# Input projection as seven block products, with attention among them and gates and convolution results in DRAM

## The chip, the cores and the metric

One core of one Trainium2 chip runs the whole kernel. The metric is the device time of one execution in microseconds; a version's time is the median of its runs. Engine names are those of the profile: PE (TensorE, matmuls), PEld (its weight loads), DVE (VectorE), ACT (ScalarE), POOL (GpSimd), SP (the queue that issues nearly all DMAs).

## The reference

A bidirectional encoder of two layers on 512 tokens of width 1024, in float32. Per layer (cut to what is computed):

```python
h = rms_norm(x, g_pre_mix[l])
z = h @ w_in[l]                                   # 1024 -> 6656 columns
q, k, v, cb, cc, cx, ga, gb = jnp.split(z, splits, axis=-1)
q = partial_rope(q.reshape(b, s, N_HEADS, HEAD_DIM), cos, sin)
k = partial_rope(k.reshape(b, s, N_KV_HEADS, HEAD_DIM), cos, sin)
y_attn = band_attention(q, k, v, attn_sink[l]) @ w_attn_proj[l]   # |i-j| <= 128
y_conv = (cb * short_conv(cc * cx, conv_w[l])) @ w_conv_proj[l]   # 3 taps
mix = (jax.nn.sigmoid(ga) * y_attn + jax.nn.sigmoid(gb) * y_conv) @ w_out[l]
x = x + rms_norm(mix, g_post_mix[l])
h = rms_norm(x, g_pre_ffn[l])
f = (jax.nn.silu(h @ w_gate[l]) * (h @ w_up[l])) @ w_down[l]
x = x + rms_norm(f, g_post_ffn[l])
```

q and the gates ga, gb have 1024 columns each, k and v 256 each, cb, cc, cx 1024 each. The FFN is 2816 wide.

## The kernel before

**Three products per float32 product.** Every matrix product is made of float32r matmuls on a high and a low part: `mm3` (L174) issues high x low, low x high, high x high into one PSUM bank. The parts of weights come from `split_w` (L129): ACT casts a 128x512 piece to its high part, DVE subtracts to get the low part. A weight tile arrives by DMA in `raw` (3 buffers), its parts lie in `hl` tiles (8 buffers of 128 x 2 x 512).

**Column tiles of 128.** A projection makes one column tile of 128 at a time for all 512 tokens: `gemm_steps` (L179) loads a 1024x128 piece of weights, splits it in two halves, and issues 8 x 3 matmuls of 512 columns. The normed input stands transposed and split in `hT` (`turn`, L238).

**A layer's mixer.** Values and keys come first (keys by `gemm_half`, two halves of 256 tokens). Then `products()` (L734) makes, for c = 0..7, a query tile (`query_tile`, L600, with rotation by `rope`), three tiles of the convolution (`conv_job`, L698: cx, cc, cb), and then eight tiles of `conv_proj` (L727). Attention is cut into `pieces` (L744 to L761): scores of a head group and block (`scores`, matmul L627, DVE L632), `softmax`, transposes and split of the weights (`weights`, L661 and L207), and the value product (`values`, L674). The loop at L770 issues a piece and then some steps of `products()`, so that pieces are spread evenly among the projections, after a lead of 12 steps. Finally, for m = 0..7, the loop at L780 makes a gate_conv tile, a gate_attn tile and a tile of the attention projection, applies the sigmoids from PSUM, and keeps the merged tile for the output projection.

**A layer's FFN.** Gate and up projections are already made as pairs of column tiles (`Pair`, L360) by a seven-product block scheme. A pair's 1024 x 256 weights are four blocks (two column tiles by two halves of the contraction); the input is four blocks too (two halves of the contraction by two halves of the tokens). Seven products of sums of such blocks, each of 4 x 3 matmuls of 256 columns, take the place of eight. `Rights` (L303) holds the sums of the input, made once; `Pair.prep` makes the sums of the weights (DVE, L393) and their parts; `Pair.product` issues the matmuls and recombines the results from PSUM (L434 to L448). `orders` sets the order of the products of all pairs. `down` (L268) is the product of the output and the down projection with the norm behind it; its last weight rows are kept resident (5 and 6 of them) and used token tile by token tile.

**What sets the order.** Each engine works its own queue in order. The order in a queue is fixed when the program is built: a scheduler places the instructions by their dependencies and its own estimate of times, starting from the order in which the code issues them, except inside `in_order` blocks. Tiles come from pools of fixed buffers (`unit` 22, `t4` 6, `t2` 6 in the code), and eight PSUM banks.

Of the kernel before, what the change touches and what calls it, by code (L numbers as in the profile page):

```python
# [10 lines left out]
F32 = mybir.dt.float32  # L11
# [18 lines left out]
EPS = 1e-6  # L30
AHEAD = 5
LEAD = 12
# [35 lines left out]
def encoder(ctx: ExitStack, tc: tile.TileContext, a, out):  # L68
# [22 lines left out]
    def unit(shape, dtype=F32R):  # L91
        return up.tile(shape, dtype, tag="u4", bufs=22, name=nm("u4"))

    def t4(shape, dtype=F32):
        return sp.tile(shape, dtype, tag="t4", bufs=6, name=nm("t4"))

    def t2(shape, dtype=F32):
        return sp.tile(shape, dtype, tag="t2", bufs=6, name=nm("t2"))
# [14 lines left out]
    cw_rows = sp.tile([DEPTH * 3 * KT, P], F32, tag="t2", bufs=6, name="cw_rows")  # L113
# [12 lines left out]
    xd = [tc.dram_tile([T, D], F32, name=f"xd{i}") for i in range(2 * DEPTH - 1)]  # L126

# [18 lines left out]
    def hl_tile():  # L146
        return wp.tile([P, 2, 512], F32R, tag="hl", bufs=8, name=nm("hl"))

    def split_cols(raw, n):

        tiles = []
        for hf in range(2):
            hl = hl_tile()
            split_w(raw[:, hf * 512 : hf * 512 + 512], hl[:, 0], hl[:, 1])
            tiles.append(hl.rearrange("p a (k c) -> p a k c", c=n))
        per = 512 // n
        return lambda part, k: tiles[k // per][:, part, k % per]
# [20 lines left out]

    def gemm_steps(w, c0, xs):  # L179
# [3 lines left out]
        for k in range(KT):  # L183
            mm3(acc, hl(0, k), hl(1, k), xs(k, 0), xs(k, 1), k == 0, k == KT - 1)
            yield
# [8 lines left out]

    def gemm(w, c0, xs):
        return run(gemm_steps(w, c0, xs))

    def gemm_half(accs, hls, xs, h):

        ts = slice(h * 256, h * 256 + 256)  # L200
        for acc, hl in zip(accs, hls):
            for k in range(KT):
                mm3(acc[:, ts], hl(0, k), hl(1, k), xs(k, 0)[:, ts], xs(k, 1)[:, ts], k == 0, k == KT - 1)
# [33 lines left out]

    def turn(t, xs, hT):  # L238

        ts = slice(t * P, (t + 1) * P)  # L240
        for hf in range(2):
            pt = bank()
            for j in range(4):
                nc.tensor.transpose(  # L244
                    pt[:, j * P : (j + 1) * P], xs[:, (4 * hf + j) * P : (4 * hf + j + 1) * P], ident
                )
            ks = slice(4 * hf, 4 * hf + 4)
            split_to(hT[:, 0, ks, ts], hT[:, 1, ks, ts], pt.rearrange("p (k c) -> p k c", k=4))
# [43 lines left out]
    def h_tile():  # L292
        return up.tile([P, 2, KT, T], F32R, tag="h", bufs=1, name=nm("h"))

    def xs_of(hT):
        return lambda k, part: hT[:, part, k, :]
# [6 lines left out]
    class Rights:  # L303


        def __init__(self):
            self.h = up.tile([P, 4, 2, KH, TH], F32R, tag="h", bufs=1, name=nm("h"))
            self.ops = {p: (self.h[:, i, 0], self.h[:, i, 1]) for i, p in enumerate((1, 2, 3, 5))}
            self.x = {}

# [9 lines left out]

        def turn(self, t, xs):
            cs = slice(t % 2 * P, t % 2 * P + P)
# [8 lines left out]

# [11 lines left out]

        def put(self, p, src, cs):
            h, lo = self.op(p)
            split_to(h[:, :, cs], lo[:, :, cs], src)
# [12 lines left out]

    class Pair:  # L360


        def __init__(self, w0, w1, c0, r):
            self.w0, self.w1, self.c0, self.r = w0, w1, c0, r
            self.hl, self.done = {}, set()

            self.raw = [None, None]

        def load(self, n, raw):
            self.raw[n] = raw  # L370
            nc.sync.dma_start(
                raw.rearrange("p (k c) -> p k c", k=KT),
                (self.w0, self.w1)[n][:, self.c0 : self.c0 + P].rearrange("(k p) c -> p k c", p=P),
            )

        def need(self, p):
            if self.raw[0] is None:
                self.load(0, raw_tile())
            if self.raw[1] is None and p not in (2, 1):
                self.load(1, unit([P, 1024], F32))  # L380

        def prep(self, p):
# [6 lines left out]
            if p not in (2, 1):  # L389
                l21, l22 = self.raw[1][:, :512], self.raw[1][:, 512:]  # L390
            if p == 5:
                self.sums = [t2([P, 512]) for _ in range(2)]
            add = lambda out, x, y: nc.vector.tensor_tensor(out=out, in0=x, in1=y, op=ALU.add)  # L393
            if p == 2:
                src = l12
            elif p == 1:
                src = l11
            elif p == 4:
                src = l22
            elif p == 5:  # L400
                src = self.sums[0]
                add(src, l21, l22)
            elif p == 6:
                src = self.sums[1]
                add(src, self.sums[0], l11)
            elif p == 3:
                src = self.sums[0]
                add(src, self.sums[1], l12)
            else:
                src = self.sums[1]  # L410
                add(src, l11, l21)
# [4 lines left out]
        def product(self, p):  # L416
# [6 lines left out]
            elif p == 1:  # L423
                self.v = t4([P, 4, TH])
                self.g = self.v[:, 2:].rearrange("p a t -> p (a t)")
            acc = self.b if p == 2 else self.c if p in (5, 3) else self.a
            hl, (h, lo) = self.hl.pop(p), self.r.op(p)
            for k in range(KH):
                mm3(acc, hl[:, 0, k], hl[:, 1, k], h[:, k], lo[:, k], p in (2, 1, 5) and k == 0, k == KH - 1, p not in (2, 1, 5))
            if p != 2:  # L430
                r1 = v2 = self.v[:, 0]
                r5 = c22 = self.v[:, 1]
# [481 lines left out]
```

## Time and profile before

| | |
|---|---|
| median of 3 runs | 1673.93 us (1673.88 to 1674.6) |
| profiled execution | 1674.66 us, its span 1672.9 us |
| mean granted PE clock | 0.997 |
| DMA | 174.35 MB, mean 104 GB/s |

The profile's page gives the busy time of each engine, the chain of work that ended last, and groups of instructions by line with their mean duration and the idle time before them. Windows of time give the same per stage: the input projection and attention of layer 0 lie between about 30 and 340 us, its FFN's pairs between about 505 and 730 us. Matmuls are pipelined, so the distance between their starts, not their duration, is what one costs. The lines that matter are shown with the prediction.

### The profile page before, as it was taken

To read this page: it belongs to the slowest core of one execution; us is meant where nothing else is said; L and a number is where in the kernel's file an instruction comes from. 1 tells how busy PE (TensorE), PEld (TensorE's weight loads), DVE (VectorE), ACT (ScalarE), POOL (GpSimd) and SP (SyncE) were. 2 spreads that over 40 slices of the span, in tenths; PEclk is the share of its full clock that TensorE was granted. 3 is DMA by queue.
4 is the path that set the end of the run, shared out by engine and by line. 5 is a ranking of instruction groups with operands and counts; after the bars stand their busy time and mean duration, and the time that the engine had idled before them with its cause. 6 is when DMAs were issued, how large, how long until landed. Compare 5 with 4: busy or idle time off the path is not lost.

```text
span 1672.9 us, 24896 instructions
## 1 busy us (share of the span) xinstructions
PE 1650.1 (99%) x9457; PEld 1454.9 (87%) x9457; DVE 1141.8 (68%) x2230; ACT 862.7 (52%) x1806; POOL 72.3 (4%) x114
## 2 busy tenths in 40 slices
PE   7999999999999999999999999999999999999998
PEld 7888888888889999988898888888888899999886
DVE  6988876434469988854469788754434899888442
ACT  5566666433346655543346666564333555556331
POOL 0000000000011100000000000000000011001000
PEclk9999999999999999999999999999999999999999
DMA  6322222433452333343413222224335333434332
GB/s 201 94 76 76 65 87 64 133 95 101 129 161 76 102 102 101 115 138 127 150 64 101 76 76 76 76 76 126 101 100 164 101 92 99 108 103 133 111 115 76
DMA packets 246937, 174.35 MB, mean 104 GB/s; under 512 B 5488, under 2 KB 232864, under 8 KB 246816
## 3 DMA queue, kind: packets, MB, share of 16 engines
q1 hardware_dynamic: 246096, 171.18, 34.6%
q8 instruction: 74, 1.21, 0.3%
q10 hardware_dynamic: 720, 1.57, 0.3%
q14 instruction: 47, 0.39, 0.1%
HBM read 164.34 MB, written 8.39 MB: 103 GB/s over the span
## 4 chain that ended last, share of the span: by engine, by line
PE 97%; DVE 2%; ACT 1%; DMA 0%; POOL 0%; issue 0%; POOLq 0%; DVEq 0%; ACTq 0%
PE bank L176 30%; PE bank L177 30%; PE bank L175 30%; PE bank L627 2%; PE bank L674 2%; PE bank L661 2%; PE bank L244 0%; DVE u L207 0%; DVE h L207 0%; DMA t<-in_x_dram 0%; ACT t L228 0%; PE bank L327 0%; DVE t L264 0%; POOL r L222 0%; DVE t L236 0%
## 5 line engine op out<-in xcount | busy, mean ns | idle before, releaser
L175 PE MATMUL bank<-h,hl 128*128 128x256 f32 (+1 forms) x1536 | 521.6, 340 | 1.1 <-DVE h L207 1.1
L176 PE MATMUL bank<-h,hl 128*128 128x256 f32 (+1 forms) x1536 | 518.2, 337 | 0.0
L177 PE MATMUL bank<-h,hl 128*128 128x256 f32 (+1 forms) x1536 | 517.8, 337 | 0.0
L131 DVE TENSOR_TENSOR hl<-raw,hl 128x512 fp32r<-128x512 f32 x428 | 292.8, 693 | 230.9 <-ACT hl L130 228.3
L130 ACT CAST hl<-raw 128x512 fp32r<-128x512 f32 x428 | 261.6, 620 | 323.4 <-PE bank L177 241.5
L177 PEld LDWEIGHTS bank<-h,hl 128*128 128x128 f32 x1536 | 292.2, 190 | 30.9
L175 PEld LDWEIGHTS bank<-h,hl 128*128 128x128 f32 x1536 | 292.5, 190 | 29.3 <-DVE h L207 1.9
L176 PEld LDWEIGHTS bank<-h,hl 128*128 128x128 f32 x1536 | 292.5, 190 | 27.6
L175 PE MATMUL bank<-u,hl 128*128 128x256 f32 (+1 forms) x784 | 251.2, 321 | 3.4 <-DVE u L207 3.4
L176 PE MATMUL bank<-u,hl 128*128 128x256 f32 (+1 forms) x784 | 250.2, 319 | 2.7 <-ACT u L206 1.8
L177 PE MATMUL bank<-u,hl 128*128 128x256 f32 (+1 forms) x784 | 250.0, 319 | 0.0
L175 PEld LDWEIGHTS bank<-u,hl 128*128 128x128 f32 x784 | 149.7, 191 | 13.8 <-DVE u L207 3.8
L176 PEld LDWEIGHTS bank<-u,hl 128*128 128x128 f32 x784 | 149.9, 191 | 13.0 <-ACT u L206 2.2
L177 PEld LDWEIGHTS bank<-u,hl 128*128 128x128 f32 x784 | 150.0, 191 | 10.3
L130 ACT CAST hl<-t 128x512 fp32r<-128x512 f32 x176 | 108.3, 621 | 58.2 <-DVE t L393 41.1
L131 DVE TENSOR_TENSOR hl<-t,hl 128x512 fp32r<-128x512 f32 x176 | 133.4, 765 | 6.0 <-ACT hl L130 3.9
L175 PE MATMUL bank<-hl,u 128*128 128x512 f32 x304 | 118.3, 389 | 0.0
L176 PE MATMUL bank<-hl,u 128*128 128x512 f32 x304 | 118.3, 389 | 0.0
L177 PE MATMUL bank<-hl,u 128*128 128x512 f32 x304 | 118.3, 389 | 0.0
L647 ACT ACTIVATE t<-t,neg 128x256 f32<-128x256 f32 (+1 forms) x128 | 70.4, 552 | 21.1 <-DVE neg L642 20.8
L632 DVE CUSTOM_DVE_ANT_0 t<-bank,tab,sink 128x256 f32<-128x256 f32 (+1 forms) x128 | 65.7, 541 | 6.1 <-PE bank L627 5.9
L448 POOL TENSOR_TENSOR u<-t 128x256 f32<-128x256 f32 x44 | 51.9, 1179 | 397.4 <-DVE t L444 236.6
(123 smaller groups left out, 2121.4 us busy)
## 6 DMA issues: line engine op xcount, KB each, us to landing
raw<-in_w_in_dram SPq DMA_DIRECT2D x104, 512.0 KB, 3.9
u<-in_w_up_dram SPq DMA_DIRECT2D x44, 512.0 KB, 5.9
raw<-in_w_down_dram SPq DMA_DIRECT2D x44, 512.0 KB, 3.5
raw<-in_w_gate_dram SPq DMA_DIRECT2D x40, 512.0 KB, 4.0
raw<-in_w_conv_proj_dram SPq DMA_DIRECT2D x16, 512.0 KB, 4.2
raw<-in_w_attn_proj_dram SPq DMA_DIRECT2D x16, 512.0 KB, 4.3
raw<-in_w_out_dram SPq DMA_DIRECT2D x16, 512.0 KB, 3.5
xd<-t SPq DMA_DIRECT2D x12, 512.0 KB, 2.9
```

The costliest lines, as they stand in the source:

```text
L130: nc.scalar.copy(h, raw)
L131: eng.tensor_tensor(out=lo, in0=raw, in1=h.bitcast(F32), op=ALU.subtract)
L175: nc.tensor.matmul(acc, wh, xl, start=first, stop=False, skip_group_check=goes_on)
L176: nc.tensor.matmul(acc, wl, xh, start=False, stop=False, skip_group_check=goes_on)
L177: nc.tensor.matmul(acc, wh, xh, start=False, stop=last, skip_group_check=goes_on)
L448: nc.gpsimd.tensor_tensor(out=out[:, TH:], in0=c22, in1=self.g[:, TH:], op=ALU.mult)
L627: nc.tensor.matmul(s[:, :w], q, kk[g][:, 1 - part, lo_b * P : lo_b * P + w], start=part == 0, stop=part == 1)
L632: nc.vector.tensor_tensor_reduce(out=p, in0=s[:, :w], in1=mask[:, m0 : m0 + w], scale=HD**-0.5, scalar=sink[:, h : h + 1], op0=ALU.add, op ...
L647: nc.scalar.activation(p, p, AF.Exp, bias=neg[:, i : i + 1], accum_out=den[:, i : i + 1])
L661: nc.tensor.transpose(pt[:, i * P : (i + 1) * P], p[:, n * P : (n + 1) * P], ident)
L674: nc.tensor.matmul(o, v, hl[:, 1 - part], start=n == 0 and part == 0, stop=kb == hi_b and part == 1)
```

## The change

- All column tiles of the input projection except the values (25 pairs a layer: keys, 4 of queries, 8 of cx with cc, 4 of cb, 8 of gate_attn with gate_conv) become `Pair`s with seven block products. `Rights` takes the place of `hT`, and keeps one more plain block so that the value tiles can read it.
- In `Pair`, two of the four sums of weight blocks move from DVE to POOL (`need`); the products issue high x low and high x high for each of four blocks first, and the four low x high matmuls at the end.
- The pair's results are recombined in SBUF and handed to a subclass: rotation for keys and queries (the product with the sine on POOL), the convolution with its first product on POOL, the product with cb on POOL, and gates.
- Gates go to DRAM (`sgd`) unprocessed and convolution results go to DRAM (`cyd`); they are loaded again ahead of the merge and of `conv_proj`.
- Attention's pieces are spread by PE time spent (`FULL`, `HALF`), up to one tile before the end; the softmax works on two heads at a time; attention results stay in float32 and are split at the end.
- Buffers: `unit` 20, `hl` 6, `t4` 6, `t2` 8, and 4 of their own for the scores. `down` keeps 4 rows resident.

Its core:

```diff
+            if self.a1 is None:
+                l11, l21, l22 = self.raw[0][:, :512], self.raw[1][:, :512], self.raw[1][:, 512:]
+                self.a1 = t2([P, 512])
+                nc.gpsimd.tensor_tensor(out=self.a1, in0=l21, in1=l22, op=ALU.add)
+                nc.gpsimd.tensor_tensor(out=l21, in0=l21, in1=l11, op=ALU.add)
...
-    def gemm(w, c0, xs):
-        return run(gemm_steps(w, c0, xs))
...
             for k in range(KH):
-                mm3(acc, hl[:, 0, k], hl[:, 1, k], h[:, k], lo[:, k], p in (2, 1, 5) and k == 0, k == KH - 1, p not in (2, 1, 5))
+                nc.tensor.matmul(acc, hl[:, 0, k], lo[:, k], start=new and k == 0, stop=False, skip_group_check=not new)
+                nc.tensor.matmul(acc, hl[:, 0, k], h[:, k], start=False, stop=False, skip_group_check=not new)
+                yield HALF
+            for k in range(KH):
+                nc.tensor.matmul(acc, hl[:, 1, k], h[:, k], start=False, stop=k == KH - 1, skip_group_check=not new)
...
-            nc.vector.tensor_tensor(out=r2, in0=r2, in1=sin, op=ALU.mult)
+            nc.gpsimd.tensor_tensor(out=r2, in0=r2, in1=sin, op=ALU.mult)
...
+        class Conv(Pair):
+            def both(self):
...
+                nc.gpsimd.tensor_tensor(out=u[:, 1 : T + 1], in0=self.out0, in1=self.out1, op=ALU.mult)
...
+        class Outer(Pair):
+            def both(self):
+                for i, acc in enumerate((self.out0, self.out1)):
+                    c = 2 * self.n + i
+                    nc.gpsimd.tensor_tensor(out=ys[c], in0=ys[c], in1=acc, op=ALU.mult)
+                    nc.sync.dma_start(cyd[l][:, c], ys[c])
...
+        class Gates(Pair):
+            def both(self):
+                nc.sync.dma_start(sgd[l][:, self.m], self.v.rearrange("p a t -> p (a t)"))
...
+        order = [Keys(r, w_in, K0, w_in, K0 + P), queries(0), conv(0), queries(1), conv(1), outer(0)]
+        for n in (1, 2, 3):
+            order += [conv(2 * n), gates(2 * n - 2), conv(2 * n + 1), outer(n), gates(2 * n - 1)]
+            if n < 3:
+                order.append(queries(n + 1))
+        order += [gates(6), gates(7)]
...
         for m in range(KT):
-            acc = gemm(w_in, GB0 + m * P, xs)
...
+            sg = t4([P, 2, T])
+            nc.sync.dma_start(sg, sgd[l][:, m].rearrange("p (a t) -> p a t", a=2))
+            nc.scalar.activation(sg, sg, AF.Sigmoid)
+            nc.gpsimd.tensor_tensor(out=sg[:, 0], in0=sg[:, 0], in1=yc[m], op=ALU.mult)
```

How it moves instructions, at three places of layer 0. On PE, in the middle of the mixer, before: a tile of the convolution (`bank_1513`, weights `hl_1507`) with the value product, transposes and scores of attention among its wide matmuls:

```order
L175 MATMUL bank_1513<-h_86,hl_1507 128x512
L176 MATMUL bank_1513<-h_86,hl_1507 128x512
L177 MATMUL bank_1513<-h_86,hl_1507 128x512
L674 MATMUL bank_1464<-t_28_1472,u_0_92 128x512 x2
L661 MATMUL bank_1532<-ident,t_25_1343 128x128 x2
L661 MATMUL bank_1532<-ident,t_27_1400 128x128 x2
L627 MATMUL bank_1541<-u_3_445,u_10_841 128x384 x2
L627 MATMUL bank_1545<-u_3_445,u_10_841 128x384 x2
```

After: one product of a pair (`bank_1216`, weights `hl_1141`), again with attention inside it:

```order
L413 MATMUL bank_1216<-h_95,hl_1141 128x256
L414 MATMUL bank_1216<-h_95,hl_1141 128x256
L759 MATMUL bank_1219<-t_10_1100,u_0_96 128x512 x2
L742 MATMUL bank_1223<-ident,ps_790 128x128 x2
L742 MATMUL bank_1223<-ident,ps_853 128x128 x2
L413 MATMUL bank_1216<-h_95,hl_1141 128x256
L414 MATMUL bank_1216<-h_95,hl_1141 128x256
...
L417 MATMUL bank_1216<-h_95,hl_1141 128x256 x4
```

The matmuls of projections are half as wide, and a product of 12 of them needs one `hl` tile, where 24 wide ones needed two.

On POOL, in the same stage, before: only the zeros at the ends of the convolution's tiles stand there.

```order
L707 MEMSET t_15_702 128x1
L708 MEMSET t_15_702 128x1
L707 MEMSET t_22_984 128x1
L708 MEMSET t_22_984 128x1
L707 MEMSET t_31_1290 128x1
```

After: sums of weight blocks (L376, L377), the sine products of the rotation (L536) and the first product of the convolution (L584), each of 512 columns.

```order
L376 TENSOR_TENSOR t_16_825<-u_29_823 128x512
L377 TENSOR_TENSOR u_29_823<-u_29_823,raw_737 128x512
L582 MEMSET t_19_961 128x1
L583 MEMSET t_19_961 128x1
L584 TENSOR_TENSOR t_19_961<-t_7_386 128x512
L536 TENSOR_TENSOR t_18_935<-t_18_935,tab 128x512
L376 TENSOR_TENSOR t_21_988<-u_31_986 128x512
L377 TENSOR_TENSOR u_31_986<-u_31_986,raw_900 128x512
L536 TENSOR_TENSOR t_23_1131<-t_23_1131,tab 128x512
```

DVE or ACT, which work in order, read the results of each of them.

On DVE, before, at a query tile (`t_26`, rotation L505 to L508, low parts L606) between softmax and weights of attention:

```order
L505 STREAM_SHUFFLE t_27_1132<-bank_1057 128x512
L506 TENSOR_TENSOR t_26_1131<-bank_1057,tab 128x512
L650 TENSOR_TENSOR rd_1106<-den_1100,es_1098 128x4
L507 TENSOR_TENSOR t_27_1132<-t_27_1132,tab 128x512
L651 RECIPROCAL rd_1106<-rd_1106 128x4
L131 TENSOR_TENSOR hl_1361<-raw_1356,hl_1361 128x512
L656 TENSOR_SCALAR t_16_1033<-t_16_1033,rd_1106 128x256
L656 TENSOR_SCALAR t_18_1087<-t_18_1087,rd_1106 128x256
L508 TENSOR_TENSOR t_26_1131<-t_26_1131,t_27_1132 128x512
```

After, at a query tile (`t_17`, rotation L534, L535, L537, low parts L562), with low parts of weights (L135), a sum of weights (L393) and the convolution (L588):

```order
L534 STREAM_SHUFFLE t_18_935<-t_8_519 128x512
L535 TENSOR_TENSOR t_17_934<-t_8_519,tab 128x512
L135 TENSOR_TENSOR hl_945<-t_16_825,hl_945 128x512
L537 TENSOR_TENSOR t_17_934<-t_17_934,t_18_935 128x512
L588 SCALAR_TENSOR_TENSOR t_20_965<-t_19_961,cw,t_20_965 128x512
L393 TENSOR_TENSOR t_16_825<-t_16_825,raw_737 128x512
L562 TENSOR_TENSOR u_30_940<-t_17_934,u_30_940 64x512 x2
```

The product with the sine (L507 before) has left DVE; its sum (L537) stands two rows behind the shuffle that POOL's product needs, and the sources of the rotation are tiles in SBUF, no longer PSUM banks.

548 lines of the change are left out of this document (285 added, 263 removed).

## The prediction

> **What bounds the kernel now.** I read the page first: the busy line and the shares of the chain of waits.
>
> ```profile
> PE 1650.1 (99%) x9457; PEld 1454.9 (87%) x9457; DVE 1141.8 (68%) x2230; ACT 862.7 (52%) x1806; POOL 72.3 (4%) x114
> PE 97%; DVE 2%; ACT 1%; DMA 0%; POOL 0%; issue 0%; POOLq 0%; DVEq 0%; ACTq 0%
> ```
>
> The chain that ends last is 97% TensorE, so today a matmul less is time less. But a busy PE is pipelined, so its price per matmul is the distance between starts, not the duration. The timeline of PE shows it for 512 columns (first two rows, twelve steps apart) and for 256 columns (last two, twelve steps apart):
>
> ```profile
> 1206.34 0.39 PE L175 MATMUL bank<-h,hl 128*128 128x512 f32 x1
> ...
> 1209.06 0.39 PE L175 MATMUL bank<-h,hl 128*128 128x512 f32 x1
> ```
> ```profile
> 701.18 0.28 PE L175 MATMUL bank<-h,hl 128*128 128x256 f32 x1
> ...
> 702.62 0.28 PE L175 MATMUL bank<-u,hl 128*128 128x256 f32 x1
> ```
>
> So 2.72/12 = 0.227 us for 512 columns and 1.44/12 = 0.120 us for 256: a half-wide matmul costs 53% of a wide one, not 50%.
>
> Then I read how near the other engines are to their limit, in the busy time by stretch: the input projection and attention of layer 0 (60 to 300), and the FFN's seven-product stage at its start and later.
>
> ```profile
> 60.00:300.00 240.00, 240.00 (x1172) 200.94 (x1171) 186.35 (x470) 155.16 (x380) 0.94 (x14) 1.00 0.27 80
> 500.00:520.00 20.00, 17.41 (x131) 16.90 (x131) 19.93 (x36) 11.50 (x23) 0.00 (x0) 0.91 0.10 28
> 540.00:560.00 20.00, 20.00 (x169) 20.00 (x168) 19.83 (x35) 11.95 (x24) 2.71 (x2) 1.00 0.33 86
> 676.00:696.00 20.00, 20.00 (x169) 20.00 (x168) 17.50 (x31) 11.35 (x23) 1.79 (x2) 1.00 0.39 106
> ```
>
> After stretch and length come PE, PEld, DVE, ACT and POOL. In the mixer DVE is busy 186 of 240 us and POOL not at all; the seven-product form, where it exists already, has DVE at 17.5 to 19.9 of 20, and where DVE reached 19.93 PE lost 2.6 us. The page's 68% for DVE is a mean over these stages: the change puts the form that fills DVE into the stage that also holds attention.
>
> **The change: TensorE.** Per layer the input projection without the values is, before, 48 column tiles of 24 wide matmuls and two key tiles of 48 half-wide ones: 1152 x 0.227 + 96 x 0.120 = 273 us. After, it is 25 pairs of 7 x 12 = 84 half-wide matmuls: 2100 x 0.120 = 252 us. That saves 20.7 us a layer (unrounded), **41.4 us** for both. Values, attention, the three other projections and the FFN keep their matmuls. The new order puts two products with the same weights one behind the other; the value product of attention does that already:
>
> ```profile
> L674 PE MATMUL bank<-t,u 128*128 128x512 f32 x160 | 50.1, 393 | 0.0
> L674 PEld LDWEIGHTS bank<-t,u 128*128 128x128 f32 x160 | 30.0, 188 | 6.3
> ```
>
> 160 matmuls in pairs with one stationary tile have 160 weight loads and the same 393 ns as others, so I give that nothing.
>
> **The change: VectorE, per layer.** The prices are these groups. Back to back each starts some 0.08 us before its predecessor ends (see the timeline below), so I take 0.08 off each mean.
>
> ```profile
> L131 DVE TENSOR_TENSOR hl<-raw,hl 128x512 fp32r<-128x512 f32 x428 | 292.8, 693 | 230.9 <-ACT hl L130 228.3
> L435 DVE TENSOR_TENSOR t<-bank,t 128x256 f32<-128x256 f32 x44 | 18.4, 418 | 8.4 <-ACT t L434 8.4
> L207 DVE TENSOR_TENSOR t<-bank,t 128x512 fp32r<-128x512 f32 x80 | 54.5, 681 | 15.2 <-ACT t L206 15.0
> L632 DVE CUSTOM_DVE_ANT_0 t<-bank,tab,sink 128x384 f32<-128x384 f32 x64 | 37.1, 608 | 0.6 <-PE bank L627 0.5
> L632 DVE CUSTOM_DVE_ANT_0 t<-bank,tab,sink 128x256 f32<-128x256 f32 x64 | 28.6, 475 | 5.5 <-PE bank L627 5.4
> L713 DVE SCALAR_TENSOR_TENSOR t<-t,cw,t 128x512 f32<-128x512 f32 x32 | 24.0, 751 | 3.3 <-ACT t L711 1.5
> L505 DVE STREAM_SHUFFLE t<-bank 128x512 f32<-128x512 f32 x20 | 14.7, 734 | 0.0
> L656 DVE TENSOR_SCALAR t<-t,rd 128x384 f32<-128x384 f32 x32 | 12.0, 418 | 0.6
> L642 DVE TENSOR_SCALAR neg<-m 128x4 f32<-128x4 f32 x32 | 5.1, 159 | 0.4
> ```
>
> - 25 pairs, each 7 low parts and 2 sums of weights at 0.60 and 3 recombinations from PSUM at 0.33: 135 + 25 = 160 us. Before, 50 tiles had 100 low parts, 60 us.
> - Rotation of 10 tiles (shuffle 0.65, cosine 0.60, sum 0.60): 18.5; low parts of queries 16 x 0.60 and keys 8 x 0.60: 14.4; convolution 16 x 0.67: 10.7.
> - Sums and low parts of the second token half: 20 x 0.60 = 12.
> - Attention: 64 score rows at 0.53 or 0.40: 30; low parts of weights 40 x 0.60: 24; 32 joins at 0.34: 11; 32 scalings at about 0.30: 10; now 128 tiny ones at 0.08: 10. Sum 85, of which 85% (72) falls between the first queries and the last pair.
>
> That is **288 us**. TensorE has in the same stretch 252 + 8 (transposes and values of the second half) + 85% of attention's 56 (80 value matmuls and 128 score matmuls at their columns' share of 0.227, 160 transposes at no more than 0.12) = **307 us**. DVE alone would be at 94%. The queue of ScalarE stays lower (155 of 240 before, three more casts of 0.5 us a pair make about 220 of 307).
>
> **The change: GpSimd.** Per layer 76 full 512-wide two-input operations (50 weight sums, 10 sine products, 16 of the convolution) enter a stage where POOL did two one-element memsets a tile. No 512-wide one is in the trace; the 256-wide one of the FFN is. First DVE, then POOL, in time order:
>
> ```profile
> 561.07 0.68 DVE L393 TENSOR_TENSOR t<-t,raw 128x512 f32<-128x512 f32 x1
> 561.67 0.68 DVE L131 TENSOR_TENSOR hl<-t,hl 128x512 fp32r<-128x512 f32 x1
> ...
> 564.68 0.68 DVE L131 TENSOR_TENSOR hl<-u,hl 128x512 fp32r<-128x512 f32 x1
> 565.28 0.41 DVE L447 SCALAR_TENSOR_TENSOR u<-bank,t 128x256 f32<-128x256 f32 x1
> 565.62 0.89 DVE L131 TENSOR_TENSOR hl<-raw,hl 128x512 fp32r<-128x512 f32 x1
> ```
> ```profile
> 561.29 4.67 POOL L448 TENSOR_TENSOR u<-t 128x256 f32<-128x256 f32 x1 [8.26 <-DVE t L444]
> ```
> ```profile
> 691.90 0.74 POOL L448 TENSOR_TENSOR u<-t 128x256 f32<-128x256 f32 x1 [8.03 <-DVE t L444]
> ```
> ```profile
> 692.05 1.15 DVE L131 TENSOR_TENSOR hl<-t,hl 128x512 fp32r<-128x512 f32 x1 [0.28 <-ACT hl L130]
> ```
>
> While DVE ran operations with two SBUF inputs back to back (starts 0.60 apart), POOL's 0.74 us took 4.67: it ended at 565.96, 0.60 after DVE's 565.36, when DVE read PSUM. The next two-input operation of DVE ended 0.55 after POOL did and lost 0.21. At 692 POOL came first and DVE's 0.68 became 1.15: 0.47 lost. So the two exclude each other, for 0.60 us per 256-wide operation, and only DVE's PSUM reads run beside it.
>
> The Trainium skill, "SBUF — State Buffer", section "SBUF: two separate sides", has the rule: GpSimd and a DVE operation with two SBUF inputs share one port pair as an exclusive lock, and the loser blocks entirely; the trace agrees (0.68 against 1.15). By that rule moving sums to GpSimd frees no DVE time, which speaks against this part of the change; with sharing at no loss the lock term below would be 0.
>
> A 512-wide hold is between 0.60 (all fixed) and 1.20 us (all proportional); I take 1.16, near the proportional end. What DVE loses of it is between 0.41 (the share 0.21/0.60) and 1.03 (0.47 + 0.56); I take 0.60, nearer the low end, because over a quarter of DVE's 288 us here (85% of attention's 30 + 24 + 11, and 25 of recombination: 80) reads PSUM, against 4 of 15 short operations in the FFN rows. That is 76 x 0.60 = **46 us** a layer (31 to 78; 0 if every hold falls into idle time of DVE).
>
> **The sum.** DVE with the lock: 288 + 46 = 334 against PE's 307, 27 over. On top, DVE waits in order for POOL inside the rotation (sum behind the sine product, ten times 1.16 = 12 at most if nothing lies between, 0 at least) and the second half's 12 us come in a burst: I take 12. So 39 a layer, 78 in all. Each stage that starts seven products behind a down projection has fewer kept rows (4, not 5 or 6: 5.4 or 10.9 us less TensorE work to hide the norms' DVE work): three such starts, 0 to 7 us each, I take 10 in all. The FFN's pairs lose two DVE sums (1.2 us) and gain two holds (0.8 to 2.1 us) in 10.1 us where DVE had 17.5 of 20: no charge. DRAM copies of gates and convolution add 32 stores and 32 loads on a share of 0.27; they are used two pairs (20 us) later, against landings of 3 to 4 us:
>
> ```profile
> raw<-in_w_in_dram SPq DMA_DIRECT2D x104, 512.0 KB, 3.9
> ...
> xd<-t SPq DMA_DIRECT2D x12, 512.0 KB, 2.9
> ```
>
> Nothing for them; if SP queued weight loads behind a late store, ten products of lead (14 us) are the cover. The profiled execution took 1674.66 us (span 1672.9), 0.7 above the median of 1673.93. **1674.7 - 41.4 + 78 + 10 = 1721 us.**
>
> **Rivals.**
> - PE stays the bound: POOL's holds fall under PSUM reads and waits of DVE. For it: 288 is under 307, and the FFN stretches ran DVE at 19.83 of 20 with PE whole. Against it: DVE must then lose under 19 us of 88 us of holds a layer, 0.25 of 1.16, less than either row above. Time 1674.7 - 41.4 = 1633, up to 1650 with starts. PE loses its place where the lost share passes 22%, and the gain is gone where holds and waits together cost 35 us a layer (19 + half of 41.4 - 10), against my 58. Ends faster. Chance 0.25.
> - Full blocking: each hold is lost whole, 76 x 1.16 = 88 a layer: 1674.7 - 41.4 + 2 x (288 + 88 + 12 - 307) + 10 = 1805. For it: 0.47 of 0.60 at 692; against: 0.21 at 565. Chance 0.08. (The Trainium skill's lock rule, named above, gives this case where no PSUM read stands beside a hold.)
> - The reordered product does more than it says: a second matmul with the same weights starts earlier. At most 0.120 - 256/512 x 0.227 = 0.007 us on each of 2632 of them, 17 us: 1616 with PE as bound. The 160 loads of 160 speak against it. Chance 0.02.
>
> **Chances and range.** Forecast 0.65, its own range 1679 (holds cost 31, waits 6, starts 10) to 1785 (78, 12, 10). 0.25 for PE as bound, 0.08 full blocking, 0.02 the weights. To hold 8 in 10 the range reaches down to 1640, into half of the first rival, and up to 1790. A measurement of this kernel can tell about 0.2% (3.3 us): faster 0.27 (first and third rival), within 0.04 (just under the forecast's lowest end), slower 0.69.
>
> **What would show it.** Right: matmuls of the pair 0.12 apart but with idle time before the first ones of a product, ended by DVE's low part; PE near 90% and DVE near full in the mixer's pair stretch; DVE's weight operations well above 693 ns; POOL about 1.2 us at best and several times that at worst. Wrong: PE at 99% there again, with DVE's groups near 690 ns; or a PE waiting for DMA landings or for a PSUM bank, which I charge nothing.

## The result, and the profile after

The changed kernel takes 1847.24 us (median of 4 runs, 1845.52 to 1850.71) against 1674.26 us (4 runs, 1673.88 to 1674.6) for the kernel before: 1.1036 times as long, 95% interval 1.1017 to 1.1055. It is 173 us slower, where 47 were forecast. The profiled execution took 1845.7 us.

The page of the changed kernel, its busy line and the shares of the chain of waits:

```profile
PE 1678.0 (91%) x11161; PEld 1548.7 (84%) x11161; DVE 1465.8 (79%) x2586; ACT 982.7 (53%) x2136; POOL 456.9 (25%) x370
PE 13%; DVE 6%; issue 1%; ACT 1%; POOL 0%; DVEq 0%; ACTq 0%; POOLq 0%
```

PE has gone from 99% busy to 91%, and the chain, whose shares sum to a fifth of the span and so could be followed back only that far, has DVE with half as much as PE. Where PE waits is in its list of waits (what PE waited for: us in total, times, longest):

```profile
PE bank L413 <- DVE t L442: 35.7, 39, 5.0
PE bank L413 <- ACT hl L134: 33.0, 20, 6.7
PE bank L413 <- DVE t L423: 19.1, 16, 6.0
PE bank L759 <- DVE t L204: 16.1, 8, 3.4
PE bank L413 <- DVE h L204: 13.3, 4, 3.9
```

Four of these rows are DVE's: L442 and L423 are recombinations, which must have read a PSUM bank before PE writes on in it, and L204 makes low parts. L134 is ACT's cast, and ACT's own list has it waiting for DVE's sum of weights most of all:

```profile
ACT hl L134 <- DVE t L393: 191.8, 94, 7.0
```

Neither a DMA nor POOL is in PE's list.

Three of the prediction's stretches at the same times, of the changed kernel (stretch, length, then PE, PEld, DVE, ACT, POOL, the granted clock, DMA share, GB/s); the second lies here ahead of the FFN's pairs, which start at 558.9, and is not to be compared:

```profile
60.00:300.00 240.00, 202.34 (x1474) 193.68 (x1472) 227.46 (x450) 140.54 (x342) 79.67 (x62) 0.91 0.27 78
540.00:560.00 20.00, 17.24 (x85) 14.27 (x84) 14.02 (x25) 11.04 (x26) 2.99 (x6) 0.96 0.38 132
676.00:696.00 20.00, 19.40 (x160) 18.99 (x160) 17.30 (x24) 10.57 (x22) 7.37 (x6) 1.00 0.32 87
```

In the mixer DVE went from 186 to 227 of 240 and PE from 240 to 202. In the FFN (676 to 696) PE has lost 0.6 of 20, where POOL has taken over two sums a pair from DVE.

To compare versions I use a stage's pair stretch: from the first to the last half-wide matmul of its pairs. For the first mixer its ends are in the view of one line (first and last start):

```profile
L413 PE MATMUL bank<-h,hl x400: 278/283/562, 21.1 to 411.0; 128*128 128x256 f32 x134
L413 PE MATMUL bank<-u,hl x300: 277/283/581, 49.8 to 416.8; 128*128 128x256 f32 x150
```

So it begins at 21.1; the last half-wide matmul follows the last of L413 and ends at 417.7. Found in this way, the two mixers and the two FFNs of the changed kernel, in order:

```profile
21.10:417.70 396.60, 337.34 (x2494) 323.28 (x2494) 375.04 (x747) 238.49 (x574) 121.36 (x93) 0.94 0.30 86
558.90:807.50 248.60, 235.19 (x1870) 230.09 (x1871) 216.02 (x313) 129.92 (x263) 88.25 (x68) 0.98 0.36 98
933.50:1327.80 394.30, 337.86 (x2495) 323.45 (x2494) 370.10 (x742) 239.14 (x573) 118.36 (x92) 0.94 0.29 85
1469.00:1719.30 250.30, 235.07 (x1870) 229.56 (x1871) 217.81 (x313) 129.89 (x263) 88.43 (x68) 0.98 0.35 95
```

and the FFNs of the kernel before:

```profile
490.90:721.40 230.50, 227.40 (x1870) 226.25 (x1871) 209.04 (x357) 138.12 (x267) 27.17 (x24) 0.99 0.39 107
1317.70:1548.20 230.50, 227.46 (x1870) 226.34 (x1871) 208.52 (x357) 136.84 (x267) 26.91 (x24) 0.99 0.38 105
```

A mixer takes 395 us where I worked out 307 of PE and 346 in all; an FFN takes 249 and 250, not 230.5. In the FFN DVE has 44 operations less (313, not 357) and is busy 7 to 9 us longer.

Which operations became longer is in the groups of DVE by line and form (count, busy us, mean ns, idle before and its releaser):

```profile
L135 DVE TENSOR_TENSOR hl<-t,hl 128x512 fp32r<-128x512 f32 x282 | 242.3, 861 | 71.9 <-ACT hl L134 70.3
L393 DVE TENSOR_TENSOR t<-t,raw 128x512 f32<-128x512 f32 x176 | 164.9, 938 | 0.7
L204 DVE TENSOR_TENSOR t<-bank,t 128x512 fp32r<-128x512 f32 x80 | 54.5, 681 | 5.1 <-ACT t L203 4.7
L718 DVE CUSTOM_DVE_ANT_0 ps<-bank,tab,sink 128x384 f32<-128x384 f32 x64 | 37.3, 607 | 0.0
```

and POOL's new ones:

```profile
L376 POOL TENSOR_TENSOR t<-u 128x512 f32<-128x512 f32 x94 | 151.1, 1612 | 170.0 <-DMA u<-in_w_in_dram 116.2 <-DMA u<-in_w_up_dram 49.7 <-ACT hl L134 3.4
L377 POOL TENSOR_TENSOR u<-u,raw 128x512 f32<-128x512 f32 x88 | 138.3, 1575 | 4.6
```

The first two groups of DVE, L135 and L393, have two inputs from SBUF. The same two forms in the kernel before, where they stand in the FFN alone:

```profile
L131 DVE TENSOR_TENSOR hl<-t,hl 128x512 fp32r<-128x512 f32 x176 | 133.4, 765 | 6.0 <-ACT hl L130 3.9
L393 DVE TENSOR_TENSOR t<-t,raw 128x512 f32<-128x512 f32 x80 | 54.4, 693 | 0.6
```

So the low parts of sums went from 765 to 861 ns and the weight sums from 693 to 938. The low parts from PSUM (681 ns) and the score rows (607) are as they were before (681 and 608). In order of time it looks like this; DVE first, then POOL:

```profile
115.15 0.16 DVE L734 TENSOR_TENSOR rd<-den,es 128x2 f32<-128x2 f32 x1
...
118.77 1.76 DVE L135 TENSOR_TENSOR hl<-t,hl 128x512 fp32r<-128x512 f32 x1
120.45 1.24 DVE L734 TENSOR_TENSOR rd<-den,es 128x2 f32<-128x2 f32 x1
121.62 0.68 DVE L537 TENSOR_TENSOR t<-t,t 128x512 f32<-128x512 f32 x1
...
131.46 1.37 DVE L135 TENSOR_TENSOR hl<-t,hl 128x512 fp32r<-128x512 f32 x1 [0.81 <-ACT hl L134]
```
```profile
120.06 1.62 POOL L377 TENSOR_TENSOR u<-u,raw 128x512 f32<-128x512 f32 x1
131.00 1.29 POOL L584 TENSOR_TENSOR t<-t 128x512 f32<-128x512 f32 x1 [9.32 <-ACT t L446]
```

L734 adds two numbers a partition. At 115 it took 0.16 us, at 120 it took 1.24: it ended at 121.69, 0.01 after POOL's sum. POOL's own 1.62 had first waited for DVE's low part, which ended at 120.53. At 131 POOL came first and ran its 1.29 us; DVE's low part of 1.37 ended at 132.83, 0.54 after POOL. The Trainium skill, "SBUF — State Buffer", section "Who interferes with whom", has it that a DVE instruction with two SBUF inputs contends with a GpSimd instruction that reads SBUF, and one with at most one SBUF input, outside the 2-port modes, doesn't. These rows agree, the tiny operation above all, and so do the unchanged groups with an input from PSUM.

### The profile page after: what moved, and what is told of

It is laid out like the page before. It is cut to its first block, busy times and chain, and to the rows that moved or that the text cites. A ratio compares the mean times of both kernels' runs of the same rounds, so it can differ in the third digit from the quotient of the medians.

```text
span 1843.9 us, 29736 instructions
## 1 busy us (share of the span) xinstructions
PE 1678.0 (91%) x11161; PEld 1548.7 (84%) x11161; DVE 1465.8 (79%) x2586; ACT 982.7 (53%) x2136; POOL 456.9 (25%) x370
## 5 line engine op out<-in xcount | busy, mean ns | idle before, releaser
L413 PE MATMUL bank<-h,hl 128*128 128x256 f32 x1504 | 392.9, 291 | 17.8 <-DVE h L204 13.3
L414 PE MATMUL bank<-h,hl 128*128 128x256 f32 x1504 | 388.4, 288 | 0.0
L413 PE MATMUL bank<-u,hl 128*128 128x256 f32 x1128 | 304.2, 299 | 88.8 <-DVE t L442 35.7
L135 DVE TENSOR_TENSOR hl<-raw,hl 128x512 fp32r<-128x512 f32 x328 | 233.8, 722 | 143.3 <-ACT hl L134 142.8
L413 PEld LDWEIGHTS bank<-h,hl 128*128 128x128 f32 x1504 | 296.7, 197 | 20.8 <-DVE h L204 14.5
L413 PEld LDWEIGHTS bank<-u,hl 128*128 128x128 f32 x1128 | 223.5, 198 | 107.0 <-DVE t L442 37.2
L135 DVE TENSOR_TENSOR hl<-t,hl 128x512 fp32r<-128x512 f32 x282 | 242.3, 861 | 71.9 <-ACT hl L134 70.3
L414 PEld LDWEIGHTS bank<-h,hl 128*128 128x128 f32 x1504 | 296.9, 197 | 0.0
L414 PE MATMUL bank<-u,hl 128*128 128x256 f32 x1128 | 293.5, 290 | 0.0
L134 ACT CAST hl<-t 128x512 fp32r<-128x512 f32 x282 | 173.5, 618 | 211.4 <-DVE t L393 191.8
L134 ACT CAST hl<-raw 128x512 fp32r<-128x512 f32 x328 | 197.8, 619 | 152.4 <-PE bank L181 113.9
L417 PE MATMUL bank<-h,hl 128*128 128x256 f32 x1504 | 248.4, 288 | 2.1 <-DVE hl L135 2.1
L414 PEld LDWEIGHTS bank<-u,hl 128*128 128x128 f32 x1128 | 224.4, 199 | 0.0
L417 PEld LDWEIGHTS bank<-h,hl 128*128 128x128 f32 x1504 | 212.9, 196 | 4.5 <-DVE hl L135 4.5
L376 POOL TENSOR_TENSOR t<-u 128x512 f32<-128x512 f32 x94 | 151.1, 1612 | 170.0 <-DMA u<-in_w_in_dram 116.2
L417 PE MATMUL bank<-u,hl 128*128 128x256 f32 x1128 | 187.9, 290 | 0.7 <-DVE hl L135 0.6
L135 DVE TENSOR_TENSOR hl<-u,hl 128x512 fp32r<-128x512 f32 x200 | 165.7, 833 | 3.8 <-ACT hl L134 2.7
L393 DVE TENSOR_TENSOR t<-t,raw 128x512 f32<-128x512 f32 x176 | 164.9, 938 | 0.7
L417 PEld LDWEIGHTS bank<-u,hl 128*128 128x128 f32 x1128 | 161.6, 199 | 1.7 <-DVE hl L135 1.7
L377 POOL TENSOR_TENSOR u<-u,raw 128x512 f32<-128x512 f32 x88 | 138.3, 1575 | 4.6
L179 PE MATMUL bank<-hl,u 128*128 128x512 f32 x352 | 137.0, 389 | 0.0
L180 PE MATMUL bank<-hl,u 128*128 128x512 f32 x352 | 137.0, 389 | 0.0
```

The costliest lines, as they stand in the source:

```text
L134: nc.scalar.copy(h, raw)
L135: eng.tensor_tensor(out=lo, in0=raw, in1=h.bitcast(F32), op=ALU.subtract)
L179: nc.tensor.matmul(acc, wh, xl, start=first, stop=False, skip_group_check=goes_on)
L180: nc.tensor.matmul(acc, wl, xh, start=False, stop=False, skip_group_check=goes_on)
L376: nc.gpsimd.tensor_tensor(out=self.a1, in0=l21, in1=l22, op=ALU.add)
L377: nc.gpsimd.tensor_tensor(out=l21, in0=l21, in1=l11, op=ALU.add)
```

## The experiments

The **theory** after reading this: each 512-wide POOL operation takes from DVE most of its hold of about 1.16 us, more than the 0.60 that DVE needs to do the same work itself, and DVE was already nearly the bound, in the mixer and in the FFN. **Rivals:** PE waits because POOL delivers late (its latency, not DVE's time); the seven-product form, its order and its starts cost the time, whatever POOL does.

### POOL's work on DVE

All six 512-wide two-input operations of POOL are issued on DVE instead:

```diff
-                nc.gpsimd.tensor_tensor(out=self.a1, in0=l21, in1=l22, op=ALU.add)
-                nc.gpsimd.tensor_tensor(out=l21, in0=l21, in1=l11, op=ALU.add)
+                nc.vector.tensor_tensor(out=self.a1, in0=l21, in1=l22, op=ALU.add)
+                nc.vector.tensor_tensor(out=l21, in0=l21, in1=l11, op=ALU.add)
...
-            nc.gpsimd.tensor_tensor(out=r2, in0=r2, in1=sin, op=ALU.mult)
+            nc.vector.tensor_tensor(out=r2, in0=r2, in1=sin, op=ALU.mult)
```

> The changed kernel (1847 us) with its 512-wide GpSimd operations (weight sums, sine products, convolution, gate merge) on VectorE instead. Theory A, the shared port: in the trace of the changed kernel VectorE's operations are 65 us longer in a mixer's pair stretch and 46 us in an FFN's than alone, so 76 operations at 0.60 us (46 us) in place of 65 us save 19 us a mixer, and the FFN goes back to about the 230 us of before (from 249): 1847 - 2 x 19 - 2 x 19 = 1771. Theory B, VectorE's own count: GpSimd's operations cost VectorE nothing, so it gains 46 us in each mixer and 26 us in each FFN: about 1990. Theory C, order and buffers (6 hl tiles, 4 kept rows): neither, 1847 within 1%.

Measured: 1744.83 us (the kernel before 1674.92 on the same chip). The windows of its first mixer and FFN:

```profile
21.30:382.30 361.00, 328.27 (x2490) 315.65 (x2490) 350.41 (x819) 237.99 (x573) 1.62 (x17) 0.96 0.32 94
524.10:758.20 234.10, 228.90 (x1870) 227.87 (x1871) 205.50 (x357) 134.01 (x263) 39.22 (x24) 0.99 0.37 104
```

The same arithmetic takes 102 us less, 26 more than theory A gave. DVE does 72 instructions more in the mixer (819, not 747) and is busy 25 us less. The Trainium skill, "Perfetto Trace Analysis", section "Optimizing Scalar/DVE Operations", says that moving operations between DVE and GpSimd might not help; here it cost 102 us. What is left, 70 us over the kernel before, is not due to the operations that had gone to POOL.

The same for the FFN's sums only:

```diff
-                nc.gpsimd.tensor_tensor(out=self.a1, in0=l21, in1=l22, op=ALU.add)
-                nc.gpsimd.tensor_tensor(out=l21, in0=l21, in1=l11, op=ALU.add)
+                self.eng.tensor_tensor(out=self.a1, in0=l21, in1=l22, op=ALU.add)
+                self.eng.tensor_tensor(out=l21, in0=l21, in1=l11, op=ALU.add)
...
         class Gated(Pair):
+            eng = nc.vector
```

> The changed kernel with the weight sums of the FFN's pairs alone on VectorE. A: the two FFN stretches fall from 249 to about 230 us, the mixers stay: 1847 - 38 = 1809. B: 44 more operations of 0.60 us on VectorE in each FFN, which fit beside TensorE's 222 us or lengthen it: 1847 to 1900. C: the FFN's 19 us come from fewer buffers and kept rows, so 1847.

Measured: 1815.84 us, 31 less. The first FFN fell from 248.6 to 234.0 and not to 230.5, so of its 18.1 us 14.6 are POOL's sums and 3.5 are something else of the change; the first mixer stayed (395.2):

```profile
557.40:791.40 234.00, 228.85 (x1870) 227.76 (x1871) 205.24 (x357) 133.82 (x263) 38.86 (x24) 0.99 0.38 104
```

### Taking POOL's work away

First POOL's two weight sums are left out of all pairs (so the weights that enter products 3, 5, 6 and 7 are not the right sums); then the sine products and both products of the convolution as well (ACT copies one input in place of the first); then DVE's two remaining weight sums too.

```diff
-                nc.gpsimd.tensor_tensor(out=self.a1, in0=l21, in1=l22, op=ALU.add)
-                nc.gpsimd.tensor_tensor(out=l21, in0=l21, in1=l11, op=ALU.add)
...
-            nc.gpsimd.tensor_tensor(out=r2, in0=r2, in1=sin, op=ALU.mult)
...
-                nc.gpsimd.tensor_tensor(out=u[:, 1 : T + 1], in0=self.out0, in1=self.out1, op=ALU.mult)
+                nc.scalar.activation(u[:, 1 : T + 1], self.out0, AF.Copy)
...
-                    nc.gpsimd.tensor_tensor(out=ys[c], in0=ys[c], in1=acc, op=ALU.mult)
```

The two sums:

> The changed kernel without the two weight sums that GpSimd makes in each pair (left out: the sum of the lower blocks, and the sum added to the lower left block; VectorE, ScalarE and TensorE keep all their instructions). A: 50 of 76 operations of GpSimd are gone from a mixer at 0.85 us each (43 us), and the FFN goes back to about 230 us: 1847 - 86 - 38 = 1723. B: VectorE has the same count, so 1847 within 1%. C: 1847.

All of it:

> As the run without the two weight sums (1716 us), and the sine products, both products of the convolution left out too (a ScalarE copy takes the place of the first), so that GpSimd has no two-input operation left in the mixers' pair stretches. Theory A, the port: the 26 remaining operations made VectorE's 23 us longer in a mixer; without them a mixer's pair stretch falls from 351 to about 328 us: 1716 - 46 = 1670. If these 26 are hidden beside reads of PSUM: 1716. VectorE's own work, with nothing beside it, is then the bound (about 310 us of work for 307 of TensorE), and TensorE should still show idle time.

DVE's sums too:

> As the run without any two-input GpSimd work in the pair stretches, and the two weight sums on VectorE left out as well (50 operations of 0.60 us a mixer, 44 an FFN). If VectorE's own count is what is left over TensorE: its work falls to about 280 us under TensorE's 307, the stretch to about 310 us and the whole to about 1632, which is the sum of matmuls saved (1674 - 41), with TensorE at 98% or more and its clock near 1.00. If something else holds TensorE (PSUM banks, loads, the order of products): no more than 10 us under the run before it.

Measured: 1716.19, 1667.97 and 1646.95 us. The first mixer of each (one fence a kernel, in this order):

```profile
21.30:372.30 351.00, 322.35 (x2492) 310.71 (x2492) 333.53 (x747) 237.74 (x573) 45.10 (x43) 0.98 0.33 97
```
```profile
21.20:348.20 327.00, 315.14 (x2492) 307.57 (x2492) 310.95 (x747) 243.83 (x582) 1.60 (x17) 0.98 0.36 104
```
```profile
21.80:341.30 319.50, 313.07 (x2492) 306.52 (x2492) 285.70 (x697) 246.43 (x581) 1.62 (x17) 0.99 0.37 106
```

From 396.6 the mixer falls by 45.6 with 50 sums gone (0.91 us each) and by 24.0 more with 26 other operations gone (0.92 each); DVE executes the same 747 instructions in the changed kernel and in the first two of these, in 375.0, 333.5 and 311.0 us. So 76 operations of POOL cost 69.6 us of time, 64.1 of them as longer busy time of DVE (0.84 each). The other 5.5 are not DVE's holds: leaving POOL's work out also removes the waits for its results, which in the changed kernel's first mixer are 4.1 us of DVE's, for the sine products, and 9.4 of ACT's:

```profile
DVE t L537 <- POOL t L536: 4.1, 3, 2.4
```

Without POOL's work in the pairs of the mixers, and without its sums in those of the FFN, with nothing put in their place, the kernel is 6 us faster than before, 0.4%: DVE's own 311 us are close to the 313 us of PE. Only with DVE's sums gone too does PE set the pace (313 of 319.5), 27 us under the kernel before and 15 above the 1632 expected.

### A hold that nobody waits for

Kernel before, with two more POOL additions in each pair of layer 1's FFN. They read the weights just loaded and write to a table that is no longer used, so nothing depends on them. In the trace no engine and no DMA issue of that stretch waits for POOL.

```diff
             if self.raw[1] is None and p not in (2, 1):
                 self.load(1, unit([P, 1024], F32))
+                for _ in range(2 if l == DEPTH - 1 else 0):
+                    nc.gpsimd.tensor_tensor(out=tab[:, :512], in0=self.raw[1][:, :512], in1=self.raw[1][:, 512:], op=ALU.add)
```

> Kernel before, with two 512-wide additions of POOL more in each of the 22 pairs of layer 1's FFN, whose result nobody reads. Theory A (a POOL operation with two SBUF inputs takes time from DVE whoever reads it): DVE has about 21 us of idle time in that stretch of 230; 44 holds at 0.9 us take 40 or more, so it grows by 15 to 30 us, the whole to 1690-1705; layer 0's FFN stays. Theory B (what costs is that products wait for POOL's late results): nobody waits, 1674 to 1676.

Measured: 1711.68 us, 36.9 over the kernel before (1674.75). Layer 0's FFN, without the additions, and layer 1's:

```profile
490.40:720.70 230.30, 227.24 (x1870) 226.24 (x1871) 209.43 (x357) 137.94 (x267) 27.12 (x24) 0.99 0.39 107
1317.00:1585.30 268.30, 237.74 (x1870) 230.27 (x1871) 246.25 (x357) 133.76 (x267) 90.38 (x64) 0.98 0.32 90
```

POOL's additions in that stretch, by line:

```profile
L382 POOL TENSOR_TENSOR tab<-u 128x512 f32<-128x512 f32 x40 | 66.1, 1653 | 66.9 <-DMA u<-in_w_up_dram 64.6
```

DVE's 357 operations take 246.25 us instead of 208.52: 37.7 us for the 40 additions within the stretch, **0.94 us each**, and the stretch is longer by the same 37.8 us. The theory holds, beyond its range: I had counted 21 us of DVE's idle time as slack that would absorb half of it, and none was absorbed (268.3 - 246.3 leaves 22 idle, as before). With PE busy 227 of 230 us and DVE 209, I read it as a stage bound by both; that reading goes beyond the run.

### POOL's sums in the kernel before

Two of the four weight sums of an FFN pair move to POOL, nothing else:

```diff
+                self.sums = t2([P, 512])
+                nc.gpsimd.tensor_tensor(out=self.sums, in0=l21, in1=l22, op=ALU.add)
+                nc.gpsimd.tensor_tensor(out=l21, in0=l21, in1=l11, op=ALU.add)
...
-                src = self.sums[0]
-                add(src, l21, l22)
```

> The kernel before (1674 us) with one part of the change alone: two of the four weight sums of an FFN pair on GpSimd. A: each FFN stretch grows as in the changed kernel, by about 19 us: 1674 + 38 = 1712. B: VectorE is relieved of 26 us in each FFN: 1674 or a few us less. C: 1674.

Measured: 1736.95 us, 62 more, where the theory gave 38. The first FFN, and the waits in it that the changed order of arrival made:

```profile
490.20:753.00 262.80, 237.06 (x1870) 228.98 (x1871) 207.01 (x313) 129.46 (x265) 86.38 (x68) 0.99 0.33 94
```
```profile
POOL t L384 <- DMA u<-in_w_up_dram: 77.2, 8, 10.4
...
ACT hl L130 <- POOL t L384: 28.5, 8, 4.7
```

DVE is busy 207, no more than before, and idle for 56 us. So here the rival has its part: POOL's sum waits for the weights to land, and ACT's cast waits for the sum. By the hold alone this stage should lose 44 x 0.94 - 44 x 0.60 = 15 us; it lost 32. The changed kernel's own FFN loses 18 and 20, close to the hold's 15; there ACT had no such wait (its 2.6 us of waits for POOL's sums all lie in the first mixer).

### Two terms by themselves

Kept rows: the kernel before with 4 instead of 5 and 6 resident rows.

```diff
-        down(a["w_out"][l], KT, 5, lambda k: (mix[k][:, 0], mix[k][:, 1]), after_mix, lambda t: r.turn(t, normed2[t]), ahead)
+        down(a["w_out"][l], KT, 4, lambda k: (mix[k][:, 0], mix[k][:, 1]), after_mix, lambda t: r.turn(t, normed2[t]), ahead)
...
-        down(a["w_down"][l], FT, 6, parts_of, after_ffn, turned)
+        down(a["w_down"][l], FT, 4, parts_of, after_ffn, turned)
```

> The kernel before with one part of the change alone: 4 kept rows in both down projections in place of 5 and 6. The prediction charged 10 us for three such starts; by theory A it costs 0 to 10: 1675 to 1685. If it costs nothing, 1674.

Measured: 1678.98 us, +5.0.

The product's order: the kernel before with two matmuls of the same weights behind each other and the low parts last, as the change has it.

```diff
-                mm3(acc, hl[:, 0, k], hl[:, 1, k], h[:, k], lo[:, k], p in (2, 1, 5) and k == 0, k == KH - 1, p not in (2, 1, 5))
+                nc.tensor.matmul(acc, hl[:, 0, k], lo[:, k], start=new and k == 0, stop=False, skip_group_check=not new)
+                nc.tensor.matmul(acc, hl[:, 0, k], h[:, k], start=False, stop=False, skip_group_check=not new)
+            for k in range(KH):
+                nc.tensor.matmul(acc, hl[:, 1, k], h[:, k], start=False, stop=k == KH - 1, skip_group_check=not new)
```

> The kernel before with one part of the change alone: in a product the matmuls with the same weights stand behind each other and those with the low part of the weights last. At 0.120 us a matmul as before: 1674 within 0.3%. If a second matmul with the same weights starts earlier (0.007 us each on 1232 of them): 1665.

Measured: 1674.35 us, no difference.

### Fewer pairs, and where

The version with all of POOL's work on DVE (but for L859's product, back on POOL), with 10 of 25 pairs of a layer made in plain column tiles of 512-wide matmuls, which ACT copies from PSUM (of the edit, the choice of pairs):

```diff
+    WHOLE = (7, 10, 11, 13, 16, 17, 19, 22, 23, 24)
...
+            for i in WHOLE:
+                whole(self.order[i])
+            self.seq = orders(len(self.order), 4, WHOLE)
```

> The changed kernel with its sums, sine and convolution products on DVE, and 10 of the 25 pairs of a layer (the gates and two pairs of queries) made in plain column tiles of 512-wide matmuls: DVE has 4 us less work in each of these, PE 0.8 more. Theory A (DVE's own count is what bounds the stretch): from the 361 of the run with all on DVE it falls to where DVE's 351 - 40 = 311 and PE's 313 + 8 meet, about 323: 1745 - 76 = 1669 (1655 to 1680). Rival (the seven-product form costs by its waits, in proportion to its pairs): 361 - 0.4 x 48 = 342: 1707.

With pairs 8, 14 and 18 of the convolution added to them:

> The same with 13 pairs in plain column tiles (three pairs of the convolution more). Theory A: DVE's 299 is now under PE's 313 + 11, the stretch about 327 with starts: 1677 (1665 to 1685), PE the bound. Rival: 361 - 0.52 x 48 = 336: 1695.

Measured: 1725.87 and 1728.18 us; both theories missed, mine by 57 and 51. The windows of the first, its mixer and three parts of it:

```profile
21.30:371.10 349.80, 328.12 (x2135) 298.98 (x2135) 306.86 (x723) 223.51 (x523) 1.61 (x17) 0.98 0.33 98
30.00:130.00 100.00, 80.72 (x585) 76.39 (x584) 97.85 (x211) 60.19 (x136) 0.40 (x6) 0.91 0.21 59
140.00:180.00 40.00, 39.62 (x273) 36.59 (x272) 35.25 (x87) 25.68 (x64) 0.00 (x0) 1.00 0.45 132
```

After 140 PE is full and DVE at 88%, as meant. But the first seven pairs are all seven products, and with the rotations, the sums of the second token half and the first score rows DVE is full from 30 to 130 while PE loses 19 us. A sum over the stage says nothing of that: my error of the prediction in small. So the last run has the same number of plain pairs, some of them early. They are not all the same ones: three pairs of the convolution take the place of two of queries and one of gates, so place and kind are not fully separated.

```diff
-    WHOLE = (7, 10, 11, 13, 16, 17, 19, 22, 23, 24)
+    WHOLE = (4, 6, 7, 8, 10, 13, 16, 19, 22, 24)
```

> The run with 10 pairs in plain column tiles had DVE at 97.9 of 100 us between 30 and 130 and PE at 80.7, and PE at 39.4 of 40 after 140. Here the same number of plain pairs, but four of them right behind the first four pairs, the others spread. Theory A (the excess is DVE's load in the first 100 us of a stage): about half of the 19 us of idle PE there and of the half clock behind them go, in both layers: 1695 (1685 to 1711). Rival (it lies elsewhere: the place of the plain pairs is of no matter): 1722 to 1730.

Measured: 1700.4 us, 25 less and inside the theory's range, with DVE's total (307) as before: the load is the same, its place is not. The same windows:

```profile
21.80:358.20 336.40, 324.22 (x2134) 297.59 (x2134) 307.21 (x725) 223.83 (x525) 1.61 (x17) 0.98 0.35 103
30.00:130.00 100.00, 87.82 (x557) 79.95 (x556) 95.44 (x206) 60.72 (x136) 0.53 (x8) 0.93 0.26 74
140.00:180.00 40.00, 40.00 (x248) 35.84 (x247) 32.61 (x86) 25.71 (x64) 0.00 (x0) 1.00 0.35 109
```

It is still 26 us behind the kernel before, and no run that computes everything beat it. The 15 pairs left save 15 x 0.83 = 12 us of PE a layer, and between 30 and 130 PE still stands 12 us (and has a clock of 0.93), which is all of its idle time in the stretch (336.4 - 324.2); in the run before it was 19 of 22. Where the rest goes I have not followed.

## Why the prediction was wrong

The direction and the mechanism were right, the size was not: 1847, outside 1640 to 1790.

- **The failed step: what DVE loses per hold.** I took 0.60 of bounds 0.41 to 1.03, because a quarter of DVE's work reads PSUM and can run beside POOL: 46 us a layer. Measured, DVE's busy time in the first mixer falls by 64 us without the 76 operations (0.84 each), and the stretch by 70 (0.92). With additions that nobody waits for it is 0.94 of both. That is inside the term's own bounds (31 to 78), near their upper end. PSUM reads are indeed untouched (681 and 607 ns). Why they save so little is argued, not shown: DVE takes its queue in order, so a two-input operation is soon at its head and waits there.
- **FFN pairs "no charge", the second failed step.** They cost 18.1 and 19.8 us, 38 together. I set the added holds against DVE's 17.5 of 20 us; the run with additions that nobody waits for shows that this idle time is no slack. Moving the sums back gave 31 us.
- **DVE's own work, 288.** It is 311 (the run without any POOL work). Some 8 us are attention: the view by line of that run has 60 of 64 score rows in the stretch, 94% of the 85 and not 85%. Another 5 are a kind of operation that I had not listed, the low parts of the reloaded convolution results, eight at 0.60. The rest is small excesses over the other items.

```profile
L714 DVE CUSTOM_DVE_ANT_0 ps<-bank,tab,sink 128x384 f32<-128x384 f32 (+1 forms) x60 | 31.6, 548 | 0.8 <-PE bank L709 0.6
...
L204 DVE TENSOR_TENSOR u<-t,u 128x512 fp32r<-128x512 f32 x8 | 5.4, 683 | 0.2 <-ACT u L203 0.2
```

- **Where PE waits.** The prediction had PE waiting for low parts of DVE, and named waiting for a PSUM bank as a sign of being wrong. The waits for recombinations (L442 and L423, 54.8 us) are of that kind, and waits for the low parts themselves (L135) come to 2.6 us in the whole list. But without POOL's work only 4.7 us of them are left, with the same banks: they are the same late DVE, seen at another operation.
- **PE's 307** is 313, for the same share of attention (94% of 56: 5 more). The saving of 41.4 was not contradicted: with the DVE sums gone as well, the kernel stood 27.0 under the one before, 5 of the other 14 us are the kept rows. In that run the two mixers' stretches are 6.4 and 6.2 us longer than PE's busy time in them and the FFNs' are 2.5 and 5.0 shorter than before (228.0 and 225.5), which leaves some 4 us that no run here settles.
- **Waits for POOL, +12 a layer.** DVE's waits for the sine products, which the term meant, are 4.1 us in the first mixer. ACT waits 9.4 us for POOL there. Of the 69.6 us that POOL's operations cost, 5.5 are not DVE's busy time, and these waits have room in that alone, so 12 was too much. In the kernel before with moved sums such a wait was real, and about as dear as the hold.
- **Starts, 10.** The kept rows cost 5.0. The dear start is another one, the first 100 us of the input projection with DVE full, which I had averaged over the stage: 25 us by the place of ten plain pairs.
- **Nothing for DRAM copies, nothing for equal weights.** No DMA is in the list of PE's waits, and the product's order by itself gave +0.4 us. The rival with shared weights falls. The stores of convolution results do hold up the queue that issues the weight loads, for which I had named a cover of 14 us. Its waits in the first mixer from 80 us on:

```profile
SPq L603 <- POOL t L602: 62.1, 8, 14.4
```

  ACT waited for the DMA of input weights for less than 8 us in the whole kernel, and POOL's sums, which waited 116.2 us for it, held up ACT for 2.6. So I take this to be nearly hidden; no run takes out the stores alone.
- **Rivals.** PE as bound (0.25) is refuted: more than 22% of each hold is lost (0.84 of 1.16). Full blocking (1805, 0.08) is the nearest in size but not by its price: 1.16 per hold against 0.84 of DVE's time and 0.92 of the stretch; it came near because the FFN and DVE's own work were left out of it.

Put together: 1674.7 - 41.4, the mixers' 83.6 and 81.3 beyond PE's 313, the FFNs' 37.9 and the kept rows' 5.0 make 1841 of the profiled 1845.7. Of a mixer's 83.6, 69.6 are POOL's operations and 14.0 are left without them (327 against 313); the sum of the prediction, 288 + 46 + 12 - 307, had 39.

## What to carry to other kernels

Moving two-input work from a busy DVE to POOL can cost DVE more than it frees: here a 512-wide addition took 0.84 to 0.94 us of DVE's time when POOL did it, and 0.60 when DVE did. DVE at 90% beside a full PE had no slack in the FFN here; price what is added there in full. And add up an engine's load by parts of a stage, not over the stage: ten plain pairs with the same total for DVE differed by 25 us by their place.

## What the runs showed that I had not expected

- An operation on two numbers a partition took 1.24 us and not 0.16 (L734) beside a 512-wide sum of POOL: a tiny blocked operation can lose as much as a large one.
- In the FFN, with PE at 99% and DVE at 91%, DVE's loss became time one to one: 37.7 us of DVE, 37.8 of the stretch, with DVE's idle time unchanged.
- Where PE starved, its granted clock fell too: 0.94 in the changed kernel's mixers, 0.99 where PE was kept busy. In the run with 10 plain pairs, the windows of 10 us where it starved:

```profile
60.00:70.00 10.00, 5.57 (x43) 4.99 (x42) 9.65 (x19) 5.92 (x11) 0.00 (x0) 1.00 0.39 105
70.00:80.00 10.00, 4.73 (x25) 4.14 (x24) 9.86 (x19) 4.52 (x8) 0.13 (x2) 0.55 0.00 0
80.00:90.00 10.00, 9.35 (x59) 8.80 (x58) 9.94 (x32) 6.66 (x20) 0.00 (x0) 0.77 0.19 54
```

PE was half idle first, at full clock, then had a clock of 0.55 and 0.77, with DVE nearly full throughout. So in these windows the lower clock comes after the starving. What it costs on top I have not measured apart.
